# Neighbourhood-attention scores: from two 128-row products on stacked halves to three 64-row products on two row tiles

## The chip, the cores and the metric

One core of one Trainium2 chip runs the whole program. The metric is the device time of one execution in microseconds (us), the median of three runs. A profiled execution of the same kernel gives the trace that all rows below come from.

## The reference, cut to what matters

The model has two layers over 256 context tokens and 1024 latent tokens of width 1024. In each layer one input projection feeds three groups of heads (an mLSTM, a neighbourhood attention, an RG-LRU); their outputs go through one output projection, and a squared-ReLU MLP follows. The change touches the neighbourhood attention alone: eight heads of width 64, with RMS-normed queries and keys.

```python
q, k, v = qkv(u_lat);  qc, kc, vc = qkv(u_ctx)          # 8 heads of 64, q and k RMS-normed
s_loc = einsum('bqhd,brqchd->bhqrc', q_r, k_win) * scale + bias   # an 8 x 16 window of latent keys
s_ctx = einsum('bqhd,bkhd->bhqk', q_r, kc) * scale                # all 256 context keys
p = softmax(concatenate([s_loc, s_ctx], -1))
o = p_loc @ v_win + p_ctx @ vc
# in layer 0 the context queries also attend to the 256 context keys
```

## The kernel before

All matrices are float32. Where a product is large, both operands are split into a high part, rounded to the matmul's reduced float32 type, and a low part, the remainder; such a product is the sum of high by high, high by low and low by high. The queries and keys of the attention follow that scheme in another form, which is what the change replaces.

**Preparation (`na_prep`, lines 660 to 713).** It runs once for each pair of heads, `hp` 0 to 3. A pair fills the 128 partitions: head 0 has partitions 0 to 63, head 1 has 64 to 127. For each of three segments of tokens, keys first and then queries, SP loads a tile `ut` from DRAM (line 681), VectorE scales it (L684), TensorE transposes it (L692 or L694) into one PSUM bank, and ScalarE and VectorE write high and low parts to SBUF. Each head has three stacks of 128 partitions: `KH` holds the high part of its keys in both halves, `KL` the low part in both halves, and `QS` the high part of its queries in its own half and the low part in the other. So ScalarE (L700, L705) and VectorE (L701, L706) run once for each head on 64 partitions, and SP copies the other halves from SBUF to SBUF (L708, L711, L712): two copies of a query segment, four of the keys.

**Scores (`na_att`).** For each pair of heads the latent queries come in eight units of 128: four column blocks `b` by two row groups `g`. A unit's scores are, for each head, 352 or 384 window keys (L834) in a bank of its own, `tL`, and 256 context keys (L838) in half of a bank that both heads share, `tC`. Each score is two products of 128 rows, `QS` by `KH` and `QS` by `KL`, which together give all four combinations of parts. In layer 0 there are also two units of context queries for each pair of heads (L780). That makes 64 latent units and 8 context units in all.

**After the scores.** VectorE adds bias and mask and finds the row maximum (L848, L852), ScalarE takes the exponential (L855), TensorE transposes the weights (L727) and multiplies them with the values (L757, the two heads on two column tiles of 64). Between the scores and these transposes each unit calls `side()`, which takes the next step of the next pair's preparation and a share of the first half of the output projection (L1363), a filler for TensorE.

**Order of the work.** A planner orders each engine's instructions from a simulated run: at each step it takes the oldest instruction in program order whose inputs and buffers are there. So the scores of a unit need not stand together on TensorE. PSUM has eight banks in five groups: `p` 1, `q` 1, `a` 3, `b` 2, `c` 1. Scores use `a`, the filler `p`, the transposes take `b`, `b`, `q` in turn (`bbq`), the output of the attention `c`. SP issues nearly all DMAs, in order.

Of the kernel before, what the change touches and what calls it, by code (L numbers as in the profile page):

```python
# [91 lines left out]
def backbone_kernel(ctx: ExitStack, tc: tile.TileContext, I, out, dbg=None):  # L92
# [522 lines left out]
    for l in range(DEPTH):  # L615
# [48 lines left out]
        def na_prep(hp, npl, stacks):  # L664


            grp = hp // 2
            h0 = (hp % 2) * 2
            QS = [npl.tile([P, NTOK], F32R, name=nm("QS"), tag="QS%d" % (hp % 2), bufs=2) for _ in range(2)]
            KH = [npl.tile([P, NTOK], F32R, name=nm("KH"), tag="KH%d" % (hp % 2), bufs=2) for _ in range(2)]  # L670
            KL = [npl.tile([P, NTOK], F32R, name=nm("KL"), tag="KL%d" % (hp % 2), bufs=2) for _ in range(2)]
            stacks += [QS, KH, KL]
            own = [slice(0, 64), slice(64, 128)]
            oth = [slice(64, 128), slice(0, 64)]
            for kd, udr, toks in (("k", u_nk, ALLT), ("q", u_nq, QT)):
                segs = [(0, 2), (2, 6), (6, 10)] if toks[0] == 0 else [(2, 6), (6, 10)]
                for (a, b) in segs:
                    n = b - a
                    w = n * P
                    ut = npl.tile([P, 4, P], F32, name=nm("ut"), tag="ut", bufs=2)  # L680
                    sp.dma_start(ut[:, :n], udr[l][a * P:b * P, hp * P:(hp + 1) * P]
                                 .rearrange("(t p) c -> p t c", p=P))
                    uv = ut[:, :n].rearrange("p t (e d) -> p t e d", e=2)
                    dve.tensor_mul(uv, uv, rsn[kd, grp][:, a:b, h0:h0 + 2].unsqueeze(3).to_broadcast([P, n, 2, 64]))  # L684
                    t = bank("b" if hp < 1 else "bbq")
                    rev = kd == "q" and a >= 2
                    for i in range(n):
                        if rev:

                            pos = n - 1 - i  # L690
                            tv = t.rearrange("p (b i c) -> p i b c", b=4, i=8)[:, 2 * pos:2 * pos + 2]
                            pe.transpose(tv, ut[:, i], flip)  # L692
                        else:
                            pe.transpose(t[:, i * P:(i + 1) * P], ut[:, i], ident)  # L694

                    o = a * P if not rev else NCTX + NLAT - (b - 2) * P
                    cs = slice(o, o + w)
                    if kd == "k":
                        for e in range(2):
                            act.activation(KH[e][own[e], cs], t[own[e], :w], AF.Copy)  # L700
                            dve.tensor_sub(KL[e][own[e], cs], t[own[e], :w], KH[e][own[e], cs].bitcast(F32))  # L701
                    else:
                        ql = npl.tile([P, 512], F32R, name=nm("ql"), tag="ql", bufs=2)
                        for e in range(2):
                            act.activation(QS[e][own[e], cs], t[own[e], :w], AF.Copy, scale=gq[own[e]])  # L705
                            dve.scalar_tensor_tensor(ql[own[e], :w], t[own[e], :w], gq[own[e]],  # L706
                                                     QS[e][own[e], cs].bitcast(F32), op0=OP.mult, op1=OP.subtract)
                            sp.dma_start(QS[e][oth[e], cs].bitcast(F32), ql[own[e], :w].bitcast(F32))  # L708
                    if kd == "k" and b == 10:
                        for e in range(2):  # L710
                            sp.dma_start(KH[e][oth[e]].bitcast(F32), KH[e][own[e]].bitcast(F32))  # L711
                            sp.dma_start(KL[e][oth[e]].bitcast(F32), KL[e][own[e]].bitcast(F32))  # L712
                    yield

        def softmax_pv(npl, S, den, tiles, vals, permT, ydst):

            PT = npl.tile([P, 2, 5, P], F32, name=nm("PT"), tag="PT", bufs=2)
            nt = len(tiles)
            if nt == 2:
                groups = [[(0, 0), (0, 1), (1, 0), (1, 1)]]  # L720
            else:
                groups = [[(0, i) for i in range(4)], [(1, i) for i in range(4)], [(0, 4), (1, 4)]]
            for gi, gr in enumerate(groups):
                t = bank("bbq")
                for j, (e, i) in enumerate(gr):
                    o, w = tiles[i]
                    pe.transpose(t[:w, j * P:(j + 1) * P], S[e][:, o:o + w], permT)  # L727
                if len(gr) == 2:
                    act.activation(PT[:, :, 4], t[:, 0:2 * P].rearrange("p (k q) -> p k q", q=P), AF.Copy)
                    continue  # L730
                if nt == 2:
                    act.activation(PT[:, :, 0:2], t.rearrange("p (e k q) -> p e k q", e=2, q=P), AF.Copy)
                    continue
                e = gi

                j = 0
                while j < 4:
                    j2 = j
                    w = tiles[j][1]
                    while j2 < 4 and tiles[j2][1] == w:  # L740
                        j2 += 1
                    src = t[:w, j * P:j2 * P].rearrange("p (k q) -> p k q", q=P)
                    if e == 0:
                        act.activation(PT[:w, e, j:j2], src, AF.Copy)
                    else:
                        dve.tensor_copy(PT[:w, e, j:j2], src)
                    j = j2

            dve.reciprocal(den, den)
            rb_ = npl.tile([P, 2, 64], F32, name=nm("rb"), tag="rb", bufs=2)  # L750
            dve.tensor_copy(rb_, den.unsqueeze(2).to_broadcast([P, 2, 64]))
            to = bank("c")
            pe.transpose(to[:, P:2 * P], rb_.rearrange("p e d -> p (e d)"), permT)
            for i in range(nt):
                w = tiles[i][1]
# [8 lines left out]
            return sm.tile([P, 2], F32, name=nm("den"), tag="den", bufs=4)  # L764
        def na_att(hp, npl, stacks, yr, side):

            QS, KH, KL = stacks

            VC = npl.tile([P, 2, P], F32, name=nm("VC"), tag="VC", bufs=1)
            uv = u_nv[l]  # L770
# [2 lines left out]
            if not last:  # L773
                for qt in range(2):
                    tS = bank("a")
                    S = []
                    den = new_den()
                    for e in range(2):
                        for i, K_ in enumerate((KH, KL)):
                            anchor = pe.matmul(tS[:, e * 256:(e + 1) * 256], QS[e][:, qt * P:(qt + 1) * P],  # L780
                                               K_[e][:, 0:256], start=(i == 0), stop=(i == 1))
                    anchors.append(anchor.ins)
                    for e in range(2):
                        s_ = npl.tile([P, 640], F32, name=nm("S"), tag="S", bufs=4)
                        nmx = sm.tile([P, 1], F32, name=nm("nmx"), tag="nmx", bufs=4)
                        mx = sm.tile([P, 1], F32, name=nm("mx"), tag="mx", bufs=4)
                        sv = tS[:, e * 256:(e + 1) * 256]
                        dve.tensor_reduce(mx, sv, axis=AX.X, op=OP.max)
                        dve.tensor_scalar(nmx, mx, -1.0, None, op0=OP.mult)
                        act.activation(s_[:, :256], sv, AF.Exp, bias=nmx, accum_out=den[:, e:e + 1])  # L790
# [11 lines left out]
            for ct, bs in enumerate(((0,), (1, 2), (3,))):  # L802
# [10 lines left out]
                for b in bs:  # L813
# [7 lines left out]
                    for g in range(2):  # L821
# [2 lines left out]
                        r0 = 0 if g == 0 else 4  # L824
                        kc = (0, 8, 24, 32)[b]
                        qo = NCTX + (1 - g) * 512 + (3 - b) * P
                        tC = bank("a")
                        tL = []
                        for e in range(2):
                            tl = bank("a")  # L830
                            tL.append(tl)
                            for i, K_ in enumerate((KH, KL)):
                                kv = K_[e][:, NCTX:].rearrange("p (r c) -> p r c", c=64)[:, r0:r0 + nr, kc:kc + 32]
                                pe.matmul(tl[:, :nl].rearrange("p (r c) -> p r c", c=32), QS[e][:, qo:qo + P], kv,  # L834
                                          start=(i == 0), stop=(i == 1))
                        for e in range(2):
                            for i, K_ in enumerate((KH, KL)):
                                anchor = pe.matmul(tC[:, e * 256:(e + 1) * 256], QS[e][:, qo:qo + P],  # L838
                                                   K_[e][:, 0:256], start=(i == 0), stop=(i == 1))
                        anchors.append(anchor.ins)  # L840
                        S = []
                        den = new_den()
                        for e in range(2):
# [5 lines left out]
                                                     in1=tab[e][:, 1 - g, 0:nl],  # L849
                                                     scale=-1.0, scalar=3.0e38, op0=OP.add, op1=OP.min,  # L850
                                                     accum_out=m1_)
                            dve.tensor_tensor_reduce(out=s_[:, nl:nl + 256], in0=tC[:, e * 256:(e + 1) * 256],  # L852
                                                     in1=zcol.to_broadcast([P, 256]), scale=-1.0, scalar=m1_,
                                                     op0=OP.add, op1=OP.min, accum_out=m2_)
                            act.activation(s_[:, :nl + 256], s_[:, :nl + 256], AF.Exp, bias=m2_, scale=-1.0,  # L855
# [739 lines left out]
```

## Time and profile before

| what | before |
|---|---|
| median of 3 runs | 3127.76 us (3114.44 to 3130.84) |
| profiled execution, its own time | 3124.27 us |
| span of the trace (first to last instruction) | 3122.5 us |
| TensorE (PE) matmul busy | 3020.2 us, 97% of the span |
| TensorE weight load (PEld) busy | 2558.1 us, 82% |
| VectorE (DVE) busy | 1900.0 us, 61% |
| ScalarE (ACT) busy | 1128.4 us, 36% |
| GpSimd (POOL) busy | 291.0 us, 9% |
| granted TensorE clock, mean | 0.988 |
| DMA | 410.73 MB, 132 GB/s over the span |

How to read it: busy time is the union of an engine's instructions. A TensorE record begins when its matmul is taken up and ends at a modelled time, and records overlap; so what a matmul costs in a dense stream is read from the step between two starts, not from its record. L834 is line 834 of the kernel; `psa<-KH,QS` is an instruction that writes a PSUM bank of group `a` and reads `KH` and `QS`; `128*128` stands for the rows and columns of the array that it uses. SPq is SyncE's queue, which issues DMAs. "Idle before" is the time for which the engine had nothing to run, with the instruction that ended it. The attention is the stretch from about 509 to 738 us in layer 0 and from about 2127 to 2347 us in layer 1.

### The profile page before, as it was taken

To read this page: it belongs to the slowest core of one execution; us is meant where nothing else is said; L and a number is where in the kernel's file an instruction comes from. 1 tells how busy PE (TensorE), PEld (TensorE's weight loads), DVE (VectorE), ACT (ScalarE), POOL (GpSimd) and SP (SyncE) were. 2 spreads that over 40 slices of the span, in tenths; PEclk is the share of its full clock that TensorE was granted. 3 is DMA by queue.
4 is the path that set the end of the run, shared out by engine and by line. 5 is a ranking of instruction groups with operands and counts; after the bars stand their busy time and mean duration, and the time that the engine had idled before them with its cause. 6 is when DMAs were issued, how large, how long until landed. Compare 5 with 4: busy or idle time off the path is not lost.

```text
span 3122.5 us, 47474 instructions
## 1 busy us (share of the span) xinstructions
PE 3020.2 (97%) x18250; PEld 2558.1 (82%) x18250; DVE 1900.0 (61%) x4318; ACT 1128.4 (36%) x2011; POOL 291.0 (9%) x252
## 2 busy tenths in 40 slices
PE   7999998999899999999999999998899999999999
PEld 6888898778788888887778889997787777887877
DVE  5757655787977667455444574765787444444444
ACT  4632223574421222233222453234564222332222
POOL 0410000222200000010000511002222000000000
PEclk8999999999999999999999999999999999999999
DMA  9624567765233444233323632347753332333233
GB/s 272 216 73 144 171 190 199 226 169 178 68 115 105 126 124 125 75 108 101 95 88 94 175 123 82 100 131 219 219 172 110 95 95 89 99 116 91 92 96 93
DMA packets 531098, 410.73 MB, mean 132 GB/s; under 512 B 27580, under 2 KB 496536, under 8 KB 530872
## 3 DMA queue, kind: packets, MB, share of 16 engines
q1 hardware_dynamic: 519448, 387.41, 41.9%
q0 software_dynamic: 8576, 15.00, 1.5%
q10 hardware_dynamic: 2848, 5.28, 0.5%
q8 instruction: 144, 2.36, 0.3%
q14 instruction: 82, 0.67, 0.1%
HBM read 339.72 MB, written 67.53 MB: 130 GB/s over the span
## 4 chain that ended last, share of the span: by engine, by line
PE 70%; DVE 11%; DMA 10%; issue 2%; ACT 2%; SPq 1%; POOL 0%; ACTq 0%; DVEq 0%; POOLq 0%
PE psa L468 14%; PE psa L1515 13%; PE psq L468 5%; PE psp L468 5%; PE psp L1515 4%; DMA mr<-in_w_mod_dram 4%; PE psq L1515 4%; PE psp L483 4%; PE psq L483 3%; PE psp L1363 3%; DVE ma L344 3%; PE psc L757 2%; PE psb L727 1%; PE psa L1363 1%; PE psa L834 1%
## 5 line engine op out<-in xcount | busy, mean ns | idle before, releaser
L200 ACT ACTIVATE wh<-wr 128x1024 fp32r<-128x1024 f32 (+3 forms) x356 | 361.8, 1021 | 929.7 <-PE psa L1515 296.3
L201 DVE TENSOR_TENSOR wl<-wr,wh 128x1024 fp32r<-128x1024 f32 (+3 forms) x356 | 424.5, 1196 | 380.6 <-ACT wh L200 374.3
L468 PE MATMUL psa<-xlo,wh 128*128 128x512 f32 (+1 forms) x856 | 319.5, 373 | 2.2 <-DVE xlo L444 2.1
L468 PE MATMUL psa<-xh,wh 128*128 128x512 f32 (+1 forms) x856 | 318.8, 373 | 2.4 <-ACT xh L443 2.4
L468 PE MATMUL psa<-xh,wl 128*128 128x512 f32 (+1 forms) x856 | 319.3, 373 | 1.4 <-DVE wl L201 1.4
L1515 PE MATMUL psa<-hl,wh 128*128 128x512 f32 (+1 forms) x768 | 286.1, 373 | 1.3 <-DVE hl L211 1.3
L1515 PE MATMUL psa<-hh,wh 128*128 128x512 f32 (+1 forms) x768 | 284.6, 376 | 0.6 <-ACT wh L200 0.5
L1515 PE MATMUL psa<-hh,wl 128*128 128x512 f32 (+1 forms) x768 | 278.1, 373 | 0.6 <-DVE wl L201 0.6
L1519 DVE SCALAR_TENSOR_TENSOR res<-psa,modt,res 128x512 f32<-128x512 f32 (+1 forms) x192 | 130.9, 693 | 165.8 <-PE psa L1515 165.6
L468 PEld LDWEIGHTS psa<-xlo,wh 128*128 128x128 f32 x856 | 161.6, 189 | 33.4 <-DVE xlo L444 2.9
L468 PEld LDWEIGHTS psa<-xh,wh 128*128 128x128 f32 x856 | 161.5, 189 | 33.4 <-ACT xh L443 2.8
L468 PEld LDWEIGHTS psa<-xh,wl 128*128 128x128 f32 x856 | 161.6, 189 | 32.5 <-DVE wl L201 2.2
L409 POOL TENSOR_TENSOR acc<-acc,nsq 128x512 f32<-128x512 f32 (+1 forms) x56 | 80.3, 1446 | 1020.6 <-ACT nsq L408 970.7
L210 ACT ACTIVATE hh<-rl 128x512 fp32r<-128x512 f32 (+1 forms) x160 | 93.5, 589 | 225.0 <-DVE rl L1491 225.0
L1515 PEld LDWEIGHTS psa<-hh,wh 128*128 128x128 f32 x768 | 144.5, 188 | 34.8 <-ACT wh L200 8.9
L483 PE MATMUL psp<-wl,xh 128*128 128x256 f32 (+1 forms) x560 | 163.1, 291 | 5.9 <-DVE wl L201 5.8
L1515 PEld LDWEIGHTS psa<-hh,wl 128*128 128x128 f32 x768 | 144.5, 188 | 28.6 <-DVE wl L201 1.5
L1515 PEld LDWEIGHTS psa<-hl,wh 128*128 128x128 f32 x768 | 144.6, 188 | 27.8 <-DVE hl L211 1.5
L483 PE MATMUL psp<-wh,xh 128*128 128x256 f32 (+1 forms) x560 | 162.2, 290 | 2.5 <-ACT wh L200 2.4
L483 PE MATMUL psq<-wh,xh 128*128 128x256 f32 (+1 forms) x560 | 162.7, 290 | 1.4 <-ACT usq L641 0.8
L483 PE MATMUL psq<-wl,xh 128*128 128x256 f32 (+1 forms) x560 | 160.9, 287 | 0.0
L483 PE MATMUL psq<-wh,xlo 128*128 128x256 f32 (+1 forms) x560 | 160.2, 286 | 0.0
(409 smaller groups left out, 7342.4 us busy)
## 6 DMA issues: line engine op xcount, KB each, us to landing
wr<-in_w_mlp_dram SPq DMA_DIRECT2D x256, 512.0 KB
mr<-in_w_mod_dram SPq DMA_DIRECT2D x92, 512.0 KB
wr<-in_w_in_dram SPq DMA_DIRECT2D x48, 512.0 KB
tab<-T_d SPq DMA_DIRECT2D x48, 384.0 KB
T_d<-E_d POOLq DMA_DIRECT2D x48, 256.0 KB, 6.5
ab<-row_d SPq DMA_DIRECT2D x36, 256.0 KB
xT_d<-res SPq DMA_DIRECT2D x4, 2048.0 KB
wr<-in_w_out_dram SPq DMA_DIRECT2D x32, 256.0 KB
```

What stands on the lines that cost most here:

```text
L200: act.activation(hi[:, a:b], raw[:, a:b], AF.Copy)
L201: dve.tensor_sub(lo[:, a:b], raw[:, a:b], hi[:, a:b].bitcast(F32))
L210: act.activation(hi, src32, AF.Copy)
L344: dve.scalar_tensor_tensor(a, raw[:, k], s[:, k], a, op0=OP.mult, op1=OP.add)
L409: pool.tensor_add(acc[bi], acc[bi], sq[:, :n])
L468: m = pe.matmul(t[:, :n], w[a][:, k, :], X[bi][b][:, k, :], start=(i == 0), stop=(i == 23))
L483: m = pe.matmul(t[:, :cols], X[bi][b][:, half * 4 + k, o:o + P], ws[half][a][:, k, :], start=(i == 0), stop=(i == 23))
L727: pe.transpose(t[:w, j * P:(j + 1) * P], S[e][:, o:o + w], permT)
L757: pe.matmul(to[64 * e:64 * e + 64, :P], vals[i][:w, 64 * e:64 * e + 64], PT[:w, e, i], start=(i == 0), stop=(i == nt - 1))
L1363: pe.matmul(t[:, :n], w[a][:, k, cc * P:(cc + 1) * P], Y[bi][b][:, k], start=(i == 0), stop=(i == 11))
L1515: m = pe.matmul(t[:, :n], w[a][:, k, cc * P:(cc + 1) * P], H[bi, k][b], start=(i == 0), stop=(i == 3 * GH - 1))
L1519: dve.scalar_tensor_tensor(xr[bi][:, ct], t[:, :n], G2[:, ct, v:v + 1], xr[bi][:, ct], op0=OP.mult, op1=OP.add)
```

## The change

Queries and keys are kept as four tiles for a pair of heads, `QH`, `QL`, `KH`, `KL`, each with head 0 in partitions 0 to 63 and head 1 in 64 to 127, two buffers each. ScalarE writes a high part and VectorE a low part once for both heads. The copies from SBUF to SBUF are gone. A score is three products of 64 rows, high by high, low by high, high by low; low by low is left out. The two heads' products alternate in the program, head 0 on the array's rows 0 to 63 and head 1 on rows 64 to 127, and each head writes banks of its own: the context scores of head 1 move from the second half of `tC` to the bank `q`. The transposes of weights and of preparation use group `b` alone.

```diff
-            QS = [... tag="QS%d" % (hp % 2), bufs=2) for _ in range(2)]   # KH, KL alike
+            QH, QL, KH, KL = (npl.tile([P, NTOK], F32R, name=nm(n_), tag=n_, bufs=2)
+                              for n_ in ("QH", "QL", "KH", "KL"))
-                    t = bank("b" if hp < 1 else "bbq")
+                    t = bank("b")
                     if kd == "k":
-                        for e in range(2):
-                            act.activation(KH[e][own[e], cs], t[own[e], :w], AF.Copy)
-                            dve.tensor_sub(KL[e][own[e], cs], t[own[e], :w], KH[e][own[e], cs].bitcast(F32))
+                        act.activation(KH[:, cs], t[:, :w], AF.Copy)
+                        dve.tensor_sub(KL[:, cs], t[:, :w], KH[:, cs].bitcast(F32))
                     else:
-                        for e in range(2):   # activation, scalar_tensor_tensor on 64 partitions, and
-                            sp.dma_start(QS[e][oth[e], cs].bitcast(F32), ql[own[e], :w].bitcast(F32))
+                        act.activation(QH[:, cs], t[:, :w], AF.Copy, scale=gq)
+                        dve.scalar_tensor_tensor(QL[:, cs], t[:, :w], gq, QH[:, cs].bitcast(F32),
+                                                 op0=OP.mult, op1=OP.subtract)
-                    if kd == "k" and b == 10:
-                        for e in range(2):
-                            sp.dma_start(KH[e][oth[e]].bitcast(F32), KH[e][own[e]].bitcast(F32))
-                            sp.dma_start(KL[e][oth[e]].bitcast(F32), KL[e][own[e]].bitcast(F32))
+        HL = ((0, 0), (1, 0), (0, 1))
+        own = [slice(0, 64), slice(64, 128)]
 # softmax_pv
-                t = bank("bbq")
+                t = bank("b")
 # latent units (the context units alike, with tS = [bank("a"), bank("q")])
-                        tC = bank("a")   # and two tl = bank("a"); per head two products of 128 rows
+                        tL = [bank("a"), bank("a")]
+                        tC = [bank("a"), bank("q")]
+                        def local(e, i):
+                            a, c = HL[i]
+                            kv = K_[c][own[e], NCTX:]...[:, r0:r0 + nr, kc:kc + 32]
+                            return pe.matmul(tL[e][:, :nl]..., Q_[a][own[e], qo:qo + P], kv, start=(i == 0), stop=(i == 2))
+                        def context(e, i):
+                            a, c = HL[i]
+                            return pe.matmul(tC[e][:, 0:256], Q_[a][own[e], qo:qo + P],
+                                             K_[c][own[e], 0:256], start=(i == 0), stop=(i == 2))
+                        for x in (local, context):
+                            for i in range(3):
+                                x(0, i)
+                                anchor = x(1, i)
```

## Rows read from the trace of the kernel before

**Rows 1.** Page, busy time, share of the span and number of instructions.
```profile
PE 3020.2 (97%) x18250; PEld 2558.1 (82%) x18250; DVE 1900.0 (61%) x4318; ACT 1128.4 (36%) x2011; POOL 291.0 (9%) x252
```

**Rows 2.** Stretches: length, busy time by engine, TensorE clock, DMA share, GB/s.
```profile
509.00:738.00 229.00, 208.18 (x1667) 176.74 (x1667) 178.94 (x565) 138.66 (x356) 45.44 (x24) 0.96 0.68 192
2127.00:2347.00 220.00, 198.25 (x1561) 162.42 (x1560) 168.98 (x506) 127.52 (x316) 55.85 (x30) 0.97 0.73 212
510.00:550.00 40.00, 30.31 (x171) 24.69 (x171) 27.22 (x71) 17.94 (x41) 8.38 (x5) 0.83 0.88 241
2130.00:2170.00 40.00, 29.07 (x154) 22.27 (x154) 27.80 (x63) 16.25 (x36) 21.05 (x11) 0.91 0.95 255
```

**Rows 3.** TensorE's timeline, scores of 352 and 256 keys: start us, us, instruction.
```profile
2172.24 0.33 PE L834 MATMUL psa<-KL,QS 128*128 128x352 f32 x1
2172.40 0.33 PE L834 MATMUL psa<-KH,QS 128*128 128x352 f32 x1
...
2172.74 0.28 PE L838 MATMUL psa<-KH,QS 128*128 128x256 f32 x1
...
2173.21 0.63 PE L1363 MATMUL psp<-yh,wh 128*128 128x512 f32 x2
2173.68 0.39 PE L1363 MATMUL psp<-yh,wl 128*128 128x512 f32 x1
```

**Rows 4.** TensorE's timeline, scores of 384 keys.
```profile
653.38 0.34 PE L834 MATMUL psa<-KL,QS 128*128 128x384 f32 x1
653.55 0.34 PE L834 MATMUL psa<-KH,QS 128*128 128x384 f32 x1
```

**Rows 5.** TensorE's timeline, layer 0's mLSTM, products on 64-row tiles (L1251).
```profile
299.20 0.72 PE L1251 MATMUL psa<-qT,kT 64*128 64x128 f32 x8
299.84 0.64 PE L316 MATMUL psc<-mr,cact 128*32 128x128 f32 x16
```

**Rows 6.** TensorE's timeline, the same stage, full tiles before and after L1251.
```profile
292.95 0.61 PE L1206 MATMUL psb<-v,kw 128*128 128x130 f32 x4
293.49 0.71 PE L1251 MATMUL psa<-qT,kT 64*128 64x128 f32 x4
294.13 0.39 PE L483 MATMUL psp<-wl,xh 128*128 128x256 f32 x1
294.36 0.27 PE L483 MATMUL psp<-wh,xlo 128*128 128x256 f32 x1
294.47 0.28 PE L483 MATMUL psp<-wh,xh 128*128 128x256 f32 x1
```

**Rows 7.** TensorE's timeline, context scores right after the column tiles of L757.
```profile
641.62 0.39 PE L838 MATMUL psa<-KH,QS 128*128 128x256 f32 x1
...
642.20 0.71 PE L727 MATMUL psb<-idj,S 128*128 128x128 f32 x5
```

**Rows 8.** TensorE's timeline, the first and the last score product.
```profile
510.33 0.36 PE L780 MATMUL psa<-KH,QS 128*128 128x256 f32 x1
...
2326.96 0.28 PE L838 MATMUL psa<-KL,QS 128*128 128x256 f32 x1
```

**Rows 9.** Chain of waits at layer 1's start: start us, us, what.
```profile
2131.85 7.75 DMA KH<-KH
2139.66 7.22 DMA QS<-ql
```

**Rows 10.** Preparation by line: count, ns min/median/max, first and last start.
```profile
L700 ACT ACTIVATE KH<-psb x36: 362/585/594, 448.3 to 2277.3; 64x512 fp32r<-64x512 f32 x24, 64x256 fp32r<-64x256 f32 x12
...
L705 ACT ACTIVATE QS<-psb,gq x30: 463/682/684, 482.8 to 2292.0; 64x512 fp32r<-64x512 f32 x24, 64x256 fp32r<-64x256 f32 x6
L706 DVE SCALAR_TENSOR_TENSOR ql<-psb,gq,QS x30: 464/740/757, 485.3 to 2294.3; 64x512 fp32r<-64x512 f32 x24, 64x256 fp32r<-64x256 f32 x6
```

**Rows 11.** DMA issues: engine, count, KB each.
```profile
KH<-KH SPq DMA_DIRECT2D x16, 320.0 KB
QS<-ql SPq DMA_DIRECT2D x32, 128.0 KB
```

More of the change, by code (lines that the diff above doesn't have):

```diff
@@ L668, in na_prep @@
             h0 = (hp % 2) * 2
[L669 to L674, printed above, removed]
+            QH, QL, KH, KL = (npl.tile([P, NTOK], F32R, name=nm(n_), tag=n_, bufs=2)
+                              for n_ in ("QH", "QL", "KH", "KL"))
+            stacks += [QH, QL, KH, KL]
             for kd, udr, toks in (("k", u_nk, ALLT), ("q", u_nq, QT)):
@@ L698, in na_prep @@
                     if kd == "k":
-                        for e in range(2):
-                            act.activation(KH[e][own[e], cs], t[own[e], :w], AF.Copy)
-                            dve.tensor_sub(KL[e][own[e], cs], t[own[e], :w], KH[e][own[e], cs].bitcast(F32))
-                    else:
-                        ql = npl.tile([P, 512], F32R, name=nm("ql"), tag="ql", bufs=2)
-                        for e in range(2):
-                            act.activation(QS[e][own[e], cs], t[own[e], :w], AF.Copy, scale=gq[own[e]])
-                            dve.scalar_tensor_tensor(ql[own[e], :w], t[own[e], :w], gq[own[e]],
-                                                     QS[e][own[e], cs].bitcast(F32), op0=OP.mult, op1=OP.subtract)
-                            sp.dma_start(QS[e][oth[e], cs].bitcast(F32), ql[own[e], :w].bitcast(F32))
-                    if kd == "k" and b == 10:
-                        for e in range(2):
-                            sp.dma_start(KH[e][oth[e]].bitcast(F32), KH[e][own[e]].bitcast(F32))
-                            sp.dma_start(KL[e][oth[e]].bitcast(F32), KL[e][own[e]].bitcast(F32))
+                        act.activation(KH[:, cs], t[:, :w], AF.Copy)
+                        dve.tensor_sub(KL[:, cs], t[:, :w], KH[:, cs].bitcast(F32))
+                    else:
+                        act.activation(QH[:, cs], t[:, :w], AF.Copy, scale=gq)
+                        dve.scalar_tensor_tensor(QL[:, cs], t[:, :w], gq, QH[:, cs].bitcast(F32),
+                                                 op0=OP.mult, op1=OP.subtract)
                     yield
+        HL = ((0, 0), (1, 0), (0, 1))
+        own = [slice(0, 64), slice(64, 128)]
         def softmax_pv(npl, S, den, tiles, vals, permT, ydst):
@@ L765, in na_att @@
         def na_att(hp, npl, stacks, yr, side):
-            QS, KH, KL = stacks
+            Q_, K_ = stacks[0:2], stacks[2:4]
             VC = npl.tile([P, 2, P], F32, name=nm("VC"), tag="VC", bufs=1)
@@ L777, in na_att @@
                     den = new_den()
[L778 to L781, printed above, removed]
+                    tS = [tS, bank("q")]
+                    for i, (a, c) in enumerate(HL):
+                        for e in range(2):
+                            anchor = pe.matmul(tS[e][:, 0:256], Q_[a][own[e], qt * P:(qt + 1) * P],
+                                               K_[c][own[e], 0:256], start=(i == 0), stop=(i == 2))
                     anchors.append(anchor.ins)
@@ L786, in na_att @@
                         mx = sm.tile([P, 1], F32, name=nm("mx"), tag="mx", bufs=4)
-                        sv = tS[:, e * 256:(e + 1) * 256]
+                        sv = tS[e][:, 0:256]
                         dve.tensor_reduce(mx, sv, axis=AX.X, op=OP.max)
@@ L826, in na_att @@
                         qo = NCTX + (1 - g) * 512 + (3 - b) * P
-                        tC = bank("a")
[L828 to L839, printed above, removed]
+                        tL = [bank("a"), bank("a")]
+                        tC = [bank("a"), bank("q")]
+                        def local(e, i):
+                            a, c = HL[i]
+                            kv = K_[c][own[e], NCTX:].rearrange("p (r c) -> p r c", c=64)[:, r0:r0 + nr, kc:kc + 32]
+                            return pe.matmul(tL[e][:, :nl].rearrange("p (r c) -> p r c", c=32),
+                                             Q_[a][own[e], qo:qo + P], kv, start=(i == 0), stop=(i == 2))
+                        def context(e, i):
+                            a, c = HL[i]
+                            return pe.matmul(tC[e][:, 0:256], Q_[a][own[e], qo:qo + P],
+                                             K_[c][own[e], 0:256], start=(i == 0), stop=(i == 2))
+                        for x in (local, context):
+                            for i in range(3):
+                                x(0, i)
+                                anchor = x(1, i)
                         anchors.append(anchor.ins)
@@ L851, in na_att @@
                                                      accum_out=m1_)
-                            dve.tensor_tensor_reduce(out=s_[:, nl:nl + 256], in0=tC[:, e * 256:(e + 1) * 256],
+                            dve.tensor_tensor_reduce(out=s_[:, nl:nl + 256], in0=tC[e][:, 0:256],
                                                      in1=zcol.to_broadcast([P, 256]), scale=-1.0, scalar=m1_,
```

## Prediction

> **What bounds the kernel now.** I read the page's busy times first: TensorE's matmul records cover 97% of the span, no other engine more than 61% [rows 1]. Since those records overlap, I went on to stretches. The reader is to see two things there. In each layer's attention TensorE is busy for 208 of 229 us and 198 of 220 us, idle for some 21 and 22, while VectorE is busy for 179 and 169 [rows 2]: TensorE sets the end, VectorE is not far behind. And half of that idle time lies in the first 40 us of each attention, 9.7 and 10.9 us, where the DMA engines are at 88% and 95% and the clock that TensorE is granted drops to 0.83 and 0.91 of full speed [rows 2]. The chain of waits says what that start is in layer 1: 7.75 us on a copy `KH<-KH` and 7.22 us on `QS<-ql`, both kinds that the change removes [rows 9]. After that I read TensorE's timeline, for steps between starts, since the question is what a score costs in a dense stream and what stands beside it.
>
> So time added to TensorE's stream counts in full, and what the other engines are spared counts only where TensorE now idles.
>
> **The products.** A product of 352 keys takes a step of 0.16 us [rows 3], one of 384 keys 0.17 [rows 4], and four of 256 keys take 0.47 [rows 3], 0.12 each. Before, a unit has four local and four context products. Afterwards it has six and six, but on two row tiles. If two heads' products run side by side, that is three steps in place of four for each kind: 0.165 + 0.12 saved, 64 latent units by 0.285 = 18, and 8 context units by 0.12 = 1. That is **-19 us**. If they run one after the other, it is six steps in place of four: +38.
>
> Which of the two holds is the first unknown. The row-tile products that the kernel already has, L1251, take 0.64 us for eight records of 128 columns [rows 5]. Two products of 512 columns take 0.47 [rows 3], so 128 columns need 0.059, and eight in a row would need 0.47: these rows allow both readings. Column tiles settle it for their kind: sixteen records of L316 take 0.64 at most [rows 5], and one after the other they would need 0.94. I take side by side, as the nearest rows that decide.
>
> The Trainium skill states more (TensorE: Matmul & The Clock Gate, "Part 3: Packing small matmuls"): tiles on different row groups run concurrently, about 4 ns apart, and four row tiles of 512 columns were measured 3.07 times as fast. By that rule the term is -19, without it +38; no row here shows it for row tiles at this width.
>
> **Entering and leaving the 64-row tiling.** This is what I see as decisive. Around L1251 the stream is not dense [rows 6]. A full-tile step there is 0.11 us (294.36 to 294.47). The four L1206 ahead take 0.54 instead of 0.44: +0.10. L1251's four pair steps (half of these records are missing) take 0.64 instead of 0.44: +0.20. The first L483 behind takes 0.23 instead of 0.12: +0.11. One visit to the row tiles costs 0.41 us. Where the neighbour is L757, on column tiles, its own change of tiling is there already: four context products after it take 0.58 [rows 7] where they take 0.47 elsewhere [rows 3]. A visit beside L757 therefore costs about half, 0.20.
>
> How many visits? I counted the stretches of score products on TensorE with nothing of another line between them, from the first at 510.33 to the last at 2326.96 [rows 8]: 71 in layer 0 and 62 in layer 1, 133 for 72 units. The planner cuts most units in two or more, because the banks come free one by one. Of the 133, 24 come right after L757 and 5 right before it. At the same order, 104 x 0.41 + 29 x 0.20 = **+48 us**. If the new order held every unit together, 72 visits with the same share of neighbours (16 and 56) cost 26. I take 48: nothing in the edit makes a bank come free earlier for the second head.
>
> **Heads apart.** In that count 44 stretches are the two local products of one head alone. Where that stays so, three products run with no partner, and the unit loses what the overlap gives, 3 x 0.165 = 0.5 us: 22 units by 0.5 = 11 at most, 0 at least. I take **+5**, the middle, as the new alternating order favours pairs.
>
> **What preparation is spared.** Two layers, four pairs of heads and three key segments make 24 key segments, and with three query segments in layer 0 and two in layer 1 there are 20 query segments. Each loses one of two ScalarE instructions, 24 of 0.585 us (L700) and 20 of 0.682 (L705), 28 us in all; VectorE loses 44 of at most 0.74, under 33 us [rows 10]. All of it lies beside TensorE's stream. DMA loses 32 copies of 320 KB (`KH` and `KL`) and 32 of 128 KB, with 8 of half that size [rows 11]: 15 MB. The attention moves 229 us x 192 GB/s + 220 x 212, 91 MB [rows 2], so a sixth less, and SP issues 72 fewer DMAs ahead of the table and value loads that queue behind them. None of it can give more than TensorE's idle time, 43 us. Less than nothing it can also not be, since only work goes. I take half of the idle time of the two starts, 10, and a quarter of the other 22: **-16 us**. What is late next at the start is the table load and the filler's weights, so not all of it goes.
>
> **Banks.** The transposes lose `q`, which now holds head 1's context scores. A group of transposes then waits at most for one more evacuation; the nearest row is L700's 0.585 us [rows 10], for 72 units 42 us, and at least nothing, as the filler stands ready. It is nearer to nothing, because a unit lasts some 5.7 us (229 us for 40 units): **+3**. The same bank `q` gives the context scores a buffer more; I put no gain on it.
>
> **Sum.** -19 + 48 + 5 - 16 + 3 = +21 on the profiled execution of 3124.27 us (a span of 3122.5 and 1.8 around it), that is 3145. The median of the runs is 3.5 us above that execution, within their spread of 16.
>
> **The rivals.**
> - *The units hold together.* With one visit for each unit the changes of tiling cost 26, all products pair (-19), and an attention that starts earlier gives 25 of its 43 idle us: -18, **3106 us**, faster. For it: the twelve products stand together in the program, and eight context products in a row exist today. Against it: banks of group `a` are released by VectorE one after the other, as before. It decides from some 85 visits downwards.
> - *It cancels.* About 100 visits (36 by the same mix), products paired, 20 of idle time given back: -3, **3121 us**. For it: VectorE, at three quarters or more of the stage, is spared some 33 us, part of which TensorE may now wait for.
> - *The row tiles give nothing.* The products of the two heads stream one after the other, or the planner sets heads so far apart that they never meet: +38 + 48 - 16 + 3 = +73, **3197 us**. For it: L1251's rows don't exclude it. Against it: the column tiles of L316.
>
> **How the numbers follow.** I give the forecast 0.50, the first rival 0.20, the second 0.17 and the third 0.13. The likeliest time is 3145; its own range is 3128 to 3165, from 100 visits to 133 with all heads apart and less idle time given back. Both signs hold weight, so the range for 8 in 10 runs from the first rival's time to half-way to the third's: 3103 to 3182. A change under 0.5%, 16 us, can't be told from none in this kernel. The forecast stands just above that bound (3143), so of its 0.50 I count 0.33 as slower and 0.17 as no change; with the rivals, slower is 0.46, no change 0.32 and faster 0.22.
>
> **What would show it.** Right: score products of form 64*128 in pairs a few ns apart, with steps of 0.12 and 0.17 for a pair; about 0.2 us at each entry and exit; more than 110 visits; the DMA total near 396 MB; no copies between the halves, and the first latent scores of layer 1 some us earlier. Wrong: fewer than 85 visits (the first rival), pairs whose second record starts a whole step later (the third), or a step into the row tiles as dense as any other. The sum would also be wrong if the granted clock fell over longer stretches than now, for which I have put no term.

## The result: 1.65% slower, and the profile after

The changed kernel takes 3177.66 us (3175.58 to 3184.56) beside 3126.13 us for the kernel before on the same chip: a ratio of 1.0165, 95% interval 1.0146 to 1.0183, or +51.5 us. The interval leaves out 1: slower, as forecast, and 33 us later than the forecast of 3145. On the page TensorE's matmul records cover as large a share of the span as in [rows 1], VectorE, ScalarE and GpSimd do a little less, and 15 MB of transfers are gone:

```profile
PE 3074.7 (97%) x18522; PEld 2560.3 (81%) x18522; DVE 1878.3 (59%) x4274; ACT 1106.0 (35%) x1967; POOL 282.5 (9%) x252
...
DMA packets 525339, 395.54 MB, mean 125 GB/s; under 512 B 26428, under 2 KB 494872, under 8 KB 525112
```

The stretches, as in [rows 2] (length, busy time by engine, TensorE clock, DMA share, GB/s). Each attention is longer, by 20 and 19 us, although VectorE and ScalarE have less to do in it; in its first 40 us the DMA engines are less full, and the granted clock is 0.91 in both layers, where [rows 2] have 0.83 and 0.91:

```profile
514.00:763.00 249.00, 234.73 (x1810) 176.70 (x1810) 162.65 (x537) 125.72 (x330) 43.46 (x24) 0.99 0.49 148
2161.00:2400.00 239.00, 220.22 (x1678) 161.10 (x1678) 156.81 (x483) 115.75 (x295) 54.00 (x30) 0.97 0.53 159
514.00:554.00 40.00, 32.56 (x199) 25.45 (x198) 22.70 (x62) 15.40 (x36) 10.86 (x6) 0.91 0.83 234
2164.00:2204.00 40.00, 32.34 (x157) 22.88 (x157) 25.94 (x49) 11.86 (x26) 19.33 (x11) 0.91 0.84 247
```

Layer 0's loss does not end with its attention. When the last value product starts, 288 of the output projection's 576 products have started, 358 before: 70 more are left behind it, some 16 us at 0.23 us each.

A unit whose products all stand together, on TensorE's timeline (start us, us, instruction), to be read beside [rows 3]:

```profile
564.80 0.27 PE L720 MATMUL psb<-idj,S 128*128 128x128 f32 x1
565.00 0.43 PE L828 MATMUL psa<-KH,QH 64*128 64x352 f32 x2
565.27 0.33 PE L828 MATMUL psa<-KH,QL 64*128 64x352 f32 x2
565.44 0.33 PE L828 MATMUL psa<-KL,QH 64*128 64x352 f32 x2
565.60 0.28 PE L833 MATMUL psa<-KH,QH 64*128 64x256 f32 x1
565.61 0.28 PE L833 MATMUL psq<-KH,QH 64*128 64x256 f32 x1
565.72 0.29 PE L833 MATMUL psa<-KH,QL 64*128 64x256 f32 x1
...
565.85 0.28 PE L833 MATMUL psa<-KL,QH 64*128 64x256 f32 x1
...
566.06 0.72 PE L1364 MATMUL psp<-yh,wh 128*128 128x512 f32 x2
566.62 0.40 PE L1364 MATMUL psp<-yh,wl 128*128 128x512 f32 x1
```

Twelve products go in six pair steps: 0.16 to 0.17 us for two of 352 keys, 0.12 for two of 256, the price of one full product before. The edges of the visit (a visit is a stretch of score products with nothing else between them) cost what was forecast: the last transpose takes 0.20 where such a step is 0.11, the first pair 0.27 for 0.16, the last pair 0.21 for 0.12, the two 512-column steps behind 0.56 for 0.47, together 0.38 us. The trace has 137 such visits (133 stretches of scores before).

What is new stands at the other end of a unit:

```profile
640.34 0.76 PE L750 MATMUL psc<-PT,VB 128*64 128x128 f32 x9 [0.50 <-DVE PT L739]
...
640.95 0.48 PE L750 MATMUL psc<-PT,VC 128*64 128x128 f32 x3
641.36 0.66 PE L689 MATMUL psb<-idj,ut 128*128 128x128 f32 x4
641.95 0.44 PE L750 MATMUL psc<-PT,VC 128*64 128x128 f32 x4
642.32 0.66 PE L720 MATMUL psb<-idj,S 128*128 128x128 f32 x4
...
643.99 0.66 PE L720 MATMUL psb<-idj,S 128*128 128x128 f32 x4
644.49 0.27 PE L746 MATMUL psc<-idj,rb 128*128 128x128 f32 x1
645.01 0.44 PE L720 MATMUL psb<-idj,S 128*128 128x128 f32 x2 [0.25 <-ACT PT L737]
```

A unit's weights are transposed in three groups, four tiles of head 0, four of head 1, and one more of each. Here the first two go out at 642.32 and 643.99, and the third, at 645.01, stands until ScalarE has copied the first (L737): there are two banks for three groups. A preparation's group (L689, 641.36) holds the other bank ahead of the second and cuts the value products of the unit before in two; over the kernel there are 125 stretches of value products in place of 83. The waits of the copying engines for transposes say how common this is (what the engine waited for: us in total, times, longest). Before, ScalarE's copy of the third group (L729) and VectorE's copy of the second (L746):

```profile
ACT PT L729 <- PE psb L727: 1.6, 4, 0.7
...
DVE PT L746 <- PE psb L727: 3.6, 7, 0.8
```

The same two copies after, L722 and L739:

```profile
ACT PT L722 <- PE psb L720: 58.8, 45, 4.9
...
DVE PT L739 <- PE psb L720: 25.0, 29, 2.5
```

I split TensorE's steps in the two attentions and their surroundings (from 440 us to the MLP's first product in layer 0, the like in layer 1) into the price of a step where nothing changes, the surplus at a change of tiling, and the rest, which is waiting. By that split 28 us of tiling changes become 86, steps grow by 14 us, and waiting falls from 111 to 98. The line between the last two moves by some 15 us with the price taken for a step, so the parts are estimates; the total, +59, doesn't (about 5 us come back in the MLP). It looked as if the tiling were the whole loss. The first experiment says otherwise.

### The profile page after: what moved, and what is told of

Same layout as the page of the kernel before. It is cut to its first block, busy times and chain, and to the rows that moved or that the text cites. A ratio compares the mean times of both kernels' runs of the same rounds, so it can differ in the third digit from the quotient of the medians.

```text
span 3175.7 us, 47763 instructions
## 1 busy us (share of the span) xinstructions
PE 3074.7 (97%) x18522; PEld 2560.3 (81%) x18522; DVE 1878.3 (59%) x4274; ACT 1106.0 (35%) x1967; POOL 282.5 (9%) x252
```

## The experiments

Times are medians, with the ratio to the kernel before on the same chip and its 95% interval; a difference is that of ratios, times 3126.

### One part alone

**e1**, the bank alone:

```diff
 # the kernel before
-                    t = bank("b" if hp < 1 else "bbq")
+                    t = bank("b")
-                t = bank("bbq")
+                t = bank("b")
```

> The kernel before, with one thing of the change: all transposes take the two banks of group b, and the bank q is left unused. Theory (the term Banks was put far too low: with two banks the planner cuts the value products on column tiles into more stretches, 136 in place of 83 by its order, and each stretch costs a change of tiling both ways, about 0.33 us): 53 x 0.33 = +17 us, about 3143; TensorE's idle time about as before, but more steps of 0.2 us around the value products. Rival, as the prediction had it (a transpose waits now and then for one evacuation, and the filler covers it): +0 to +3 us, 3126 to 3129.

3179.72 us, 1.0168 (1.0147 to 1.0189): +53 us. Both expectations were far too low. This edit costs as much as the whole change. Its waits are like those of the change:

```profile
ACT PT L729 <- PE psb L727: 66.8, 39, 4.4
...
DVE PT L746 <- PE psb L727: 22.4, 18, 3.9
```

**e4**, no copies between halves (SP's copies taken out, `memset` of the other halves put in):

> The kernel before without its copies between the halves: the other halves of the stacks are set to zero on GpSimd, so low by high and low by low parts are left out of the scores; ScalarE and VectorE still run once for each head, the products and banks are as before. Theory (the term for spared preparation, -16, held): -10 to -16 us, 3110 to 3116, with fewer idle us in the first 40 us of each attention. Rival (transfers are hidden anyway; TensorE finds other work while it waits): -0 to -3 us, 3123 to 3126.

3118.82 us, 0.9971 (0.9959 to 0.9984): -9 us. The relief exists, at half of what I had put.

**e3**, full rows in place of row tiles:

```diff
 # from the changed kernel; QH, QL per head with the other half zero
-  pe.matmul(tS[e]..., Q_[a][own[e], ...], K_[c][own[e], ...], ...)
+  pe.matmul(tS[:, e * 256:(e + 1) * 256], Q_[a][e][:, ...], K_[c][:, ...], ...)   # all scores alike
+  # tC one bank for both heads, transposes on b and bbq, as before
```

> No row tiles: each head's queries lie in a tile of 128 rows whose other half is zero, keys of both heads stacked, three products of 128 rows for each score; no copies between halves, banks and transposes as before (three transposes banks, both heads' context scores in one bank). It has six products in a row where before had four and the change has three pair steps. Theory (the tiling is what costs; the products alone are +38 us by the rows, and the spared preparation gives back about 13): 3126 + 38 - 13 = 3151, so faster than the change although no two products overlap. Rival (the row tiles pay for themselves, and the change loses elsewhere, in banks): 3126 + 38 and no relief, 3164, or more, up to 3190, slower than the change.

3135.88 us, 1.0033 (1.0020 to 1.0045): +10 us, and +19 over e4, for products that add 38 us of steps. So about half of what is added to TensorE's stream seems to go into waits that it has anyway; e3 also splits the keys once for both heads, which e4 does not, so the 19 is not of the products alone.

**e2**, the units held together:

```diff
-                        for x in (local, context):
-                            for i in range(3):
-                                x(0, i)
-                                anchor = x(1, i)
+                        lead = context(1, 0)
+                        with tc.issue_after(lead.ins):   # then the other eleven, context first
```

> The changed kernel with the twelve products of a latent unit held together: head 1's first context product, which needs the bank that comes free last, goes first, and the other eleven are ordered behind it, so every product finds its partner of the other head; the planner's order has 80 stretches of score products in place of 137, and as many stretches of value products as the change, 124. Theory (stretches and products without a partner are what the forecast had too small): 57 x 0.36 = 20 us less for the tiling and some 15 to 18 us less for lone products, against a few us of waiting for banks: 3137 to 3145. Rival (the loss comes from the supply of banks; a unit that waits for its last bank loses in waits what it spares in steps): 3170 to 3180, as the change.

3174.66 us, 1.0151 (1.0130 to 1.0172). With 80 visits and nearly every product in its pair (432 steps of score products, 552 in the change) it is 4 us faster than the change, inside the intervals. With two banks, visits are not what sets the time.

### Do the terms add up?

**e5**, row tiles for the local scores alone, banks as before (from e3: `local` on `Q_[a][e][own[e]]` and `K_[c][own[e]]`, heads alternating):

> Row tiles with the banks as before: the local scores are three 64-row products per head on two row tiles, in the two banks that they had before; the context scores are three products of 128 rows on zero-padded queries, both heads in one bank as before; transposes have b, b, q; no copies. Theory now (the third bank of the transposes is the whole loss of the change; steps that the row tiles add go mostly into waits that TensorE has anyway, as the 38 us of full products did, of which 17 were seen): from 3119 without copies, plus 6 us of products and 40 to 45 us of tiling changes, of which a third to a half is seen: 3133 to 3145. Rival (the terms add up, and the tiling costs its full 40 to 45): 3165 to 3170.

3150.16 us, 1.0086 (1.0069 to 1.0104): +27, between the two, and 17 over e3. The prediction's terms fit here: the local products take 277 steps, 192 if all were paired and 384 if none, so the overlap saves 18 us against e3; 100 visits of 0.4 cost 40; together +22.

**e6**, e3 with all transposes on group `b`:

> The kernel with three products of 128 rows on padded queries (no row tiles, no copies), with all transposes on the two banks of group b as in the change; q unused. It differs from the change only in how the products are laid on the array and in head 1's context bank. Theory now (with two banks the waits for banks set the pace, and TensorE's steps fill them, whichever they are): 3172 to 3182, the same as the change within 0.3%. Rival (terms add up: 53 us for the banks on the 3136 of full rows with three banks): 3185 to 3195.

3190.17 us, 1.0216 (1.0195 to 1.0236): +57 over e3. The rival was right: the bank costs the same 53 to 57 us with the products of before (e1) and with six full ones (e6). With all scores on row tiles and a third bank to spare no run was made. Beside the change, full rows are 16 us slower with these banks.

**e7**, the change with `bank("bbq")` for the weights' transposes:

> The changed kernel with the weights' transposes on b, b, q again; q then serves both them and head 1's context scores. The planner's order cuts the scores into 192 stretches (137 in the change) and the values into 145 (125). Theory now (transposes that wait for a bank are the loss): faster than the change, 3145 to 3170, though it has 75 more tiling visits. Rival (tiling visits are the loss, 0.35 us each): 3178 + 27 = 3205.

3209.31 us, 1.0291 (1.0266 to 1.0317). The rival's number, but it tells little: it has most stretches of both kinds (192 and 145), and `q` is held by head 1's scores while transposes want it.

**e8**, only the weights' transposes lose `q`:

> The kernel before, with the weights' transposes on the two banks of group b and the preparation's on b, b, q as before: one half of the bank loss of 53 us. Theory now (72 units bring some 200 groups of weights' transposes, the preparation 44 groups, and the waits go with the groups): 3126 + 35 to 50 = 3161 to 3176. Rival (it is the preparation's groups that block, since each of their banks is held for two slow evacuations, 0.6 and 0.74 us, and a queue of transposes stands behind): 3126 to 3140.

3154.56 us, 1.0099 (1.0081 to 1.0117): +31 of the 53, below the theory's range; the other 22 come with the preparation's groups.

### Repairs that failed

**e9, e10, e11**: the third group in the free half of `c`, in the change, in e2 and in the kernel before.

```diff
+                if len(gr) == 2:
+                    to = bank("c")
+                    t = to[:, 256:512]
+                else:
+                    t = bank("b")        # "bbq" in the kernel before
...
-            to = bank("c")
+            if nt == 2:              # context units
+                to = bank("c")
```

> The changed kernel with one edit: a unit's third group of transposes (one tile of each head, 256 columns) is written into the free half of the unit's output bank c, so only two groups a unit cycle through the two banks of group b. The planner's order has 73 stretches of value products in place of 125 and 136 of scores in place of 137. Theory (what the lost bank costs is the wait of the third group, and with it the value products cut in two): the 53 us come back, 3123 to 3133. Rival (the units are paced by the number of banks as a whole; c is now held longer, from the transposes to the output's evacuation): 3165 to 3185.

> The same edit on the grouped version of the change (head 1's first context product ahead, the other eleven behind it): 83 stretches of scores, nearly all products beside their partner, 73 stretches of values. Theory (terms add up when no bank is waited for: 53 fewer tiling visits of 0.36 us, and about 18 us of lone steps): 15 to 30 us below the ungrouped version with the same edit, 3098 to 3115, so below the kernel before. Rival (as with two banks, where grouping gave 3 us: waits for score banks take what the steps give): within 5 us of the ungrouped version.

> The kernel before with the same edit alone: third group of transposes in the free half of c, the other two on b, b, q. 74 stretches of values in place of 83. Theory (even with three banks some groups wait for a bank; 1.1 us for each stretch of values, as the runs with two banks showed): 3126 - 10 = 3116, range 3106 to 3121. Rival (three banks are enough, and c held longer costs): 3126 to 3140.

3171.25 us, 1.0148 (1.0129 to 1.0168); 3175.19, 1.0155 (1.0137 to 1.0174); 3173.30, 1.0150 (1.0130 to 1.0169). My theory fell: the value products are whole again (73, 73 and 74 stretches) and nothing comes back; the kernel before even loses 47 us. Since the repair itself costs as much there, these runs can't tell what the cut value products cost. The single bank `c` now has to serve a unit from its transposes to its output, and the third group's copy still waits for its transposes, 24 us in e9 and 16 in e11; that this is the new loss is argued, not shown.

**e12**, e11 with `KL`'s other halves zero in place of copied:

> The kernel before with that edit, and with the other halves of KL set to zero in place of copied, so low by low is left out as in the change and 16 copies of 320 KB go. Theory (copies are worth some 8 us in all, and these are about a third of their bytes): 2 to 4 us below the version with the edit alone, 3103 to 3119. Rival (the remaining copies, KH and QS, which the chain of waits showed, are all that counts): no difference from the version with the edit alone, within 2 us.

3159.30 us, 1.0100 (1.0081 to 1.0118): 16 us below e11, more than all copies were worth in e4. Why it is so much here stays open.

**e13, e14**, VectorE's copy of the second group moved to ScalarE, in the change and before:

```diff
-                    if e == 0:
-                        act.activation(PT[:w, e, j:j2], src, AF.Copy)
-                    else:
-                        dve.tensor_copy(PT[:w, e, j:j2], src)
+                    act.activation(PT[:w, e, j:j2], src, AF.Copy)
```

> The changed kernel with the copies of head 1's transposed weights (three a unit, 64 units) on ScalarE in place of VectorE, so VectorE never stands before a group of transposes. Theory (with two banks VectorE waits in order for transposes, 13 us in layer 1's attention, and the score evacuations behind it keep banks of group a): 15 to 30 us faster than the change, 3148 to 3163, with the first read of local scores back from 4.1 to some 3.2 us after the last product. Rival (the group's own wait for a bank is what counts, whoever copies; ScalarE gets a longer queue): 3173 to 3190.

> The same edit on the kernel before, with three banks: a control. VectorE's waits for transposes are small there (under 3 us), so by the theory the edit only shifts some 40 us of work from VectorE (179 of 229 us busy) to ScalarE (139): -10 to +3 us, 3116 to 3130. Rival (ScalarE, the longer queue, becomes the late one): +8 to +25.

3181.05 us, 1.0161 (1.0146 to 1.0175), and 3129.11, 0.9992 (0.9981 to 1.0004). No difference in either: that VectorE stands in its queue is a sign of the wait, not its price. Nor is the sum of the copies' waits for transposes the price. It falls by half, from 111 us in the change to 53 in e13, where ScalarE alone copies (L736 both heads' groups, L722 the third):

```profile
ACT PT L736 <- PE psb L720: 30.2, 34, 4.1
ACT PT L722 <- PE psb L720: 19.9, 22, 3.2
```

The count of cut value products doesn't set the time alone either: e13 has 149 stretches of values, the change 125.

**e15**, the preparation's transposes in the filler's bank (`bank("b" if hp < 1 else "p")`):

> The changed kernel with the preparation's transposes (of the second to fourth pair of heads) in the filler's bank p, so that the two banks of group b serve the weights' transposes alone. Theory (in the kernel before two fifths of the bank loss, 21 of 53 us, lay with the preparation's groups): 3178 - 20 = 3158, range 3148 to 3168. Rival (the filler, which needs p, is then held up, and the weights' three groups still do not fit two banks): 3173 to 3195.

3175.36 us, 1.0137 (1.0121 to 1.0153): 9 us back of the 20 expected.

### Two groups for two banks

**e16, e17, e18**: the kernel before, e1 and the change, each with two groups of transposes for a unit. They leave out the last 128 context keys in the weights' transposes and the value products, so they spare that work too and don't compute the model; only their differences are used.

```diff
-                groups = [[(0, i) for i in range(4)], [(1, i) for i in range(4)], [(0, 4), (1, 4)]]
+                groups = [[(0, i) for i in range(4)], [(1, i) for i in range(4)]]
...
-                        tiles = [...] + [(nl, P), (nl + P, P)]     # vals alike
+                        tiles = [...] + [(nl, P)]
```

> The kernel before with two groups of transposes for a latent unit in place of three: the last 128 context keys are left out of the weights' transposes and of the value products (two transposes, two pairs of value products and one copy less for each of 64 units). Baseline for the next two. By TensorE's steps 64 x (2 x 0.1 + 0.11) = 20 us less: 3100 to 3112.

> The same with all transposes on the two banks of group b. Theory (a unit's third group, which can not be written before its first is copied out, is the loss): 0 to 15 us above the run before it, against 53 with three groups. Rival (the banks in general are short; the preparation's groups stand between as well): 25 to 50 us above it.

> The changed kernel with two groups of transposes for a latent unit, the same part left out; it differs from the run before it in the products, the score banks and the preparation alone. Theory (these add up to nothing: 51 for the change less 53 for the bank): within 8 us of the run before it. Rival (the row tiles' changes of tiling, 44 us by the steps, were hidden in waits for banks and now show): 20 to 40 us above it.

3106.23 us, 0.9935 (0.9919 to 0.9950); 3120.43, 0.9980 (0.9971 to 0.9989); 3132.61, 1.0019 (1.0008 to 1.0029). With two groups the third bank is worth 14 us in place of 53: the theory held here, at the upper end of its range. The edit also sends 8 tiles in place of 10 through the banks, so a shortage that grows with the load, and not with the third group as such, is not excluded. VectorE's wait is nearly that of before, in e17

```profile
DVE PT L746 <- PE psb L727: 5.1, 8, 1.1
```

and in e18

```profile
DVE PT L739 <- PE psb L720: 5.8, 10, 1.4
```

The rest of the change then costs 12 us (e18 less e17), between the theory's 8 and the rival's 20. Its order is not that of the change: 157 visits and 645 steps of score products for 137 and 552. No version that computes all the scores' terms of the change and all values was faster than the kernel before; e14 equals it.

## Why the prediction was right in sign and short by 33 us

- **The step that failed is "Banks".** It let a group wait "at most for one more evacuation", 0.585 us for 72 units, put +3 between 0 and 42 because "the filler stands ready" and "a unit lasts some 5.7 us", and is +53 measured alone (e1), above its upper end. What it missed is a count: three groups a unit go through `b`, `b`, `q` with hardly a wait, and through `b`, `b` the third waits for the first's copy. With two groups the loss is 14 (e17). The price is shown, and that most of it goes with the third group; how the wait spreads from there is only seen, in the copies' waits (58.8 and 25.0 us) and in local scores that VectorE takes up later (first read 4.1 us after the last product in layer 0's attention, 3.0 before, means of 64; but in layer 1's it is 3.4 in both). Three repairs at single points of that spread gave nothing or 9 us.
- **Products, -19**: the pairs and their steps came as forecast, so the rival of one stream after the other is out. [Rows 5] and [rows 6] could have told: L1251 has 144 records, two for each of its 72 products, so none is missing. A visit of eight records takes 0.64 us, and so does one of four. At the 0.11 that the prediction itself takes for such a record, eight one after the other would need 0.88; its 0.059 is taken from another kind of product. **Heads apart, +5**, was mis-sized: the score products take 552 steps where 408 would do if all were paired (544 before), so 144 steps have no partner, the overlap's gain is down to about 1 us, and this term is some 18, above the 11 put as its most.
- **Entering and leaving, +48**: 137 visits for 133 forecast, 0.38 us at the unit shown; by my split the changes cost 58, of which 42 more stretches of values make about 15. Right, as far as the split goes.
- **Spared preparation, -16**: -9 (e4). The start is as forecast: copies gone, layer 0's first score at 485.13 us among the input projection's products (510.33 before [rows 8]), the first latent score of layer 1 at 2166.72 us, 5 us after the projection's last product (16 before), and then other waits come.
- **"Time added to TensorE's stream counts in full"** was too strict: 38 us of products showed as some 19 (e3 against e4). TensorE's records overlap, so the idle time between them, 43 us in the two attentions, understates its waits: by the steps they are some 111 us in the wider stretches of the split.
- **The sum.** Without the bank my terms are +18, and e18 against e17 measures +12. That these are close is luck: with e18's own counts (237 steps without a partner, 157 visits) my prices and e4's -9 give some +57, an estimate. With the bank the sum would be 53 + 12 = 65, and 51.5 came: the row tiles' extra steps seem to fall partly into the waits for banks, as e1's waits, 36 us above those of before by the split, are 13 below them in the change. Taking the third group out brings 59 us in e1 and 45 in the change, where 20 are its own work (e16): beyond that it costs 39 in e1 and 25 in the change. So that e1 alone equals the change is partly chance, and the bank's share of the change's 51.5 is not isolated. The measured time lies in the range for 8 in 10, 3103 to 3182, but the upper end of that came from the third rival, which is out. The chances as listed add up to 0.34 for no change and 0.20 for faster, not 0.32 and 0.22. **The rival of units that hold together** set the point at 85 visits; e2 has 80 and gains 4 us. It overlooked the same bank.

The Trainium skill (Trainium Kernel Development and Optimization, "Best Practices") says that tiling TensorE speeds up compute but not the emptying of PSUM. The trace agrees: pairs run at the price of one product, and ScalarE's copy of a third group takes 0.384 us after and 0.378 before. That the copies' speed sets the time is not shown; e13 and e14 moved copies to another engine and changed nothing.

## What to carry to other kernels

Before an edit takes a bank from a stage, count the groups that one unit writes into the banks that remain. Here one group more than there were banks cost 53 us where the length of one copy for each unit had given at most 42, so price such a wait by an experiment. Try the bank alone in the old kernel first; here that two-line edit would have given the sign and, partly by chance, the size. And count a row-tile product's gain only for those that stand beside their partner in the order that the planner gives, with what a visit costs at its edges, 0.4 us here.

## What the hardware showed beside that

In this trace row tiles take up their products independently of one another, out of program order. In this stretch the program has head 1's three local products ahead of head 0's three context products (TensorE's timeline):

```profile
655.47 0.44 PE L828 MATMUL psa<-KH,QH 64*128 64x384 f32 x1
655.48 0.38 PE L833 MATMUL psa<-KH,QH 64*128 64x256 f32 x1
655.70 0.28 PE L833 MATMUL psa<-KH,QL 64*128 64x256 f32 x1
655.75 0.34 PE L828 MATMUL psa<-KH,QL 64*128 64x384 f32 x1
655.82 0.28 PE L833 MATMUL psa<-KL,QH 64*128 64x256 f32 x1
655.93 0.34 PE L828 MATMUL psa<-KL,QH 64*128 64x384 f32 x1
656.10 0.28 PE L833 MATMUL psq<-KH,QH 64*128 64x256 f32 x1
656.22 0.28 PE L833 MATMUL psq<-KH,QL 64*128 64x256 f32 x1
656.34 0.28 PE L833 MATMUL psq<-KL,QH 64*128 64x256 f32 x1
```

Head 0's first two context products start at 655.48 and 655.70, before head 1's second local product at 655.75, which the program has ahead of them; each tile goes at its own step (0.12 for 256 keys, 0.18 for 384). Head 1's context products, whose partners had gone, take a full step of 0.12 each alone. The Trainium skill (TensorE: Matmul & The Clock Gate, "Part 3: Packing small matmuls") holds that packed matmuls start and end strictly in program order; this trace shows another order, and the measurement decides. So in this trace two heads needn't alternate in the program to overlap; it was enough that both had products in the same visit.
